# Turning rows of x by VectorE blocks and transfers within SBUF, in a hybrid decoder layer

## The chip, the core and the metric

The kernel runs on one core of a Trainium2 chip. The metric is the device time of one execution in microseconds (us), lower is better. TensorE (PE) multiplies and transposes, VectorE (DVE) and ScalarE (ACT) do elementwise work and empty PSUM, GpSimd (POOL) and SyncE (SP) mostly issue transfers (DMAs). SBUF is the memory on the chip with 128 partitions, PSUM the accumulator memory of TensorE.

## What is computed

The reference is one decoder layer on x, 2048 tokens by 1024 channels in float32:

```python
h = _rmsnorm(x, norm1_w)
proj = h @ w_in                                  # 1024 -> 3840 columns
o_hg = _hgrn2_mixer(...)                         # 4 heads of 128: gated linear recurrence over tokens
o_rw = _rwkv7_mixer(...)                         # 8 heads of 64: recurrence with a data-dependent decay
x = x + concatenate([o_hg, o_rw]) @ w_out
x = x + _conv_ffn(_rmsnorm(x, norm2_w), w_up, conv_w, conv_b, w_down)
out = _rmsnorm(x, final_norm_w)
```

The change touches the first line alone: how h reaches the layout in which TensorE multiplies it with w_in. That product needs channels on the partitions and tokens along the free dimension, while x lies in memory with one token per row.

## The kernel before

**Stages.** The first stage (up to about 1300 us) does the first norm, the input projection, both recurrences and the output projection of token blocks 0 to 2. The second does the rest. The change lies in the first stage, in the function `phase1`.

**Blocks.** The 2048 tokens are four blocks of 512 (`NBLK`, `BLK`). `KD` is 8: the 1024 channels are eight groups of 128. For each block, `hh` and `hl` hold the normed and turned h as a high and a low part, 128 channels by 512 tokens for each of the eight groups k. A projection of 128 columns is 8 x 3 matmuls (`mm3`, L270 to L272) into one PSUM bank of the kind "pj", of which there are two.

**Three streams.** `dense()` yields the projections, `rw_stream()` the rwkv recurrence (units `rw_super`, two per block) and `hg_stream()` the hgrn2 heads (`hg_unit`). A loop takes one step of each recurrence and then fills with 2000 ns of dense work, by the costs that `dense()` yields. So the program's order comes about. A planner then puts each engine's instructions in order: of those that are ready by its own costs it takes the one that comes first in the program. Each engine and each queue afterwards runs its list strictly in that order.

**The job list.** `dense()` builds a list of jobs: for each block a mark ("A"), then 30 projections ("P"), and ahead of blocks 2 and 3 the output projection of block 0 and 1 ("O"). `at[nb]` is the place of the mark of block nb. Into this list go extra jobs, at places counted from `at[nb]`: "E" jobs, which only issue work and cost nothing in the count, and jobs that yield costs. For the next block these are

- at +18 `load4`: four transfers of 128 rows of x (512 KB each) into `rows[nb]`, a tile "xt" of 128 partitions x 4 x 1024, one buffer;
- at +22 `norm4`: sums of squares (ScalarE, into a "wraw" buffer) and scaling of the rows (VectorE, L431);
- at +25 the job "T", `turn`: for each k four transposes of 128x128 on TensorE (L443) into a "pj" bank, which ScalarE copies back in place over the rows of `rows[nb]`, so that the tile then holds channels on its partitions.

In the last projection of the block (block 0), or in the last quarter of the output projection that follows it, `next_block` calls `split_h` for each k (L451, L452): the turned rows times the norm's weights, split into `hh` and `hl`.

**Block 0** is turned another way (`transposed`, with eviction straight into `hh`), at the start. Rows of x1 for the second norm (keys `("N", nb)`) also come through `load4` and are turned by `transposed`.

**Buffers that matter.** The pool `wp` has four buffers "wraw" of 2 KB per partition. In block 0 the weights pass through them: each projection loads two raw tiles of w_in (L568, issued by POOL), ScalarE and VectorE split them into "wh" and "wl", and POOL stores the split weights to memory (`Win`), from where later blocks load them without "wraw". The norm's squares, the rows of h for the second norm and the raw w_out tiles of the output projection use "wraw" too.

**SP's queue.** `dma` issues on SP. In the first stage SP carries, besides the loads of x: in each `rw_super` the transfers of `KBT` (16), `Ed` (4), `E` (2) and `RHS` (16), the first and last of which finish turns that VectorE began with 32x32 block transposes (L754, L765); the stores of the mixers' outputs to `oT`; and in the output projections the loads of `oT` ("oraw", L388) and x and the stores of x1. The step-by-step solve in `rw_super` (L804, L806) waits for `E`.

Of the kernel before, what the change touches and what calls it, by code (L numbers as in the profile page):

```python
# [7 lines left out]
F32 = mybir.dt.float32  # L8
# [3 lines left out]
AF = mybir.ActivationFunctionType  # L12
# [6 lines left out]
P = 128  # L19
T = 2048  # L20
D = 1024
KD = D // P
BLK = 512
# [44 lines left out]
def tile_layer(ctx, tc, consts, x, norm1_w, w_in, hg_lb_logits, hg_norm_w, rw_shift_mu, rw_w0, rw_w2,  # L68
# [4 lines left out]
    V, S, TE = nc.vector, nc.scalar, nc.tensor  # L73
# [40 lines left out]
    def act(out_, in_, func, **kw):  # L114

        want = tables.get(func)
        if want is not None and want != tab["now"]:
            pre = S.preload_act_table_set(want)
            for u_ in tab["uses"]:
                tc.add_manual_dep(pre.ins, u_.ins.name, NOSYNC, reason="table order")  # L120
            tab.update(now=want, pre=pre, uses=[])
        i_ = S.activation(out_, in_, func, **kw)  # L122
        if want is not None:
            tc.add_manual_dep(i_.ins, tab["pre"].ins.name, NOSYNC, reason="table order")
            tab["uses"].append(i_)
        return i_
# [147 lines left out]
    def phase1(c1):  # L274
# [22 lines left out]
        def bank(kind):  # L297
            return ps.tile([P, 512], F32, tag=kind, name=kind, bufs=2)
# [121 lines left out]
        def load4(key, src, r0):  # L420
            def f():
                rows[key] = row_tile()
                for i in range(4):
                    dma(rows[key][:, i, :], src[r0 + i * P:r0 + (i + 1) * P, :])
            return f

        def norm4(key):
            def f():
                for i in range(4):
                    t_ = rows[key][:, i, :]  # L430
                    V.tensor_scalar_mul(t_, t_, rstd(wp, t_, "nst", "wraw", 4))  # L431
            return f
# [1 line left out]
        def four_tiles(t_):  # L434
            return [t_[:, i, :] for i in range(4)]

        def turn(nb):

            t_ = rows[nb]
            for k in range(KD):  # L440
                tp = bank("pj")
                for i in range(4):
                    TE.transpose(tp[:, i * P:(i + 1) * P], t_[:, i, k * P:(k + 1) * P], ident)  # L443
                act(t_[:, :, k * P:(k + 1) * P], tp.rearrange("p (i t) -> p i t", i=4), AF.Copy)
                yield 436

        def split_h(nb, k):

# [67 lines left out]
        def dense():  # L516

            rows[0] = first
            jobs = []
            for nb in range(NBLK):  # L520
                if nb >= 2:
                    jobs.append(("O", nb - 2))
                jobs.append(("A", nb))
                jobs.append(("P", 3584, ev_lora(nb), lambda nb=nb: done["rw1"] >= 2 * nb, None))
                for s_ in range(2):
                    if s_ == 1:
                        jobs.append(("P", 3712, ev_gd(nb), lambda nb=nb: done["rw2"] >= 2 * nb, None))
                    n_rw = 2 * nb + s_
                    for u in range(3):
                        for p in (2 * s_, 2 * s_ + 1):  # L530
                            jobs.append(("P", 2048 + u * 512 + p * P, ev_rkv(nb, p, u),
                                         lambda n=n_rw: done["rw1"] >= n,
                                         mark("rw") if (u == 2 and p == 2 * s_ + 1) else None))
                    for j in (2 * s_, 2 * s_ + 1):
                        n_hg = 4 * nb + j
                        for i, ev in enumerate((ev_q, ev_f, ev_v, ev_g)):
                            jobs.append(("P", i * 512 + j * P, ev(nb, j), lambda n=n_hg: done["hg"] >= n - 1,
                                         mark("hg") if i == 3 else None))
            jobs.append(("O", 2))


            at = [i for i, jb in enumerate(jobs) if jb[0] == "A"]
            extra = []
            for nb in range(NBLK):
                if nb + 1 < NBLK:
                    extra += [(at[nb] + 18, ("E", load4(nb + 1, x[0], (nb + 1) * BLK))),
                              (at[nb] + 22, ("E", norm4(nb + 1))), (at[nb] + 25, ("T", nb + 1))]
                if nb >= 2:
                    extra += [(at[nb] + 6, ("E", load4(("N", nb - 2), x1d[nb - 2], 0))),
                              (at[nb] + 10, ("E", norm4(("N", nb - 2)))), (at[nb] + 11, ("N", nb - 2))]  # L550
            for m in range(2):
                extra += [(at[3] + 14 + 5 * m, ("E", sum_load(m))), (at[3] + 17 + 5 * m, ("E", sum_make(m)))]
            extra += [(at[3] + 25 + m, ("W", 2, o_take(m))) for m in range(4)]
            for i, jb in sorted(extra, key=lambda e: e[0], reverse=True):
                jobs.insert(i, jb)
            cols = [jb[1] for jb in jobs if jb[0] == "P"]
            NCOL = len(cols) // NBLK
            Win = [[[dp.tile([P, 4, P], F32, name=f"Win{ct}{k2}{c}") for c in "hl"] for k2 in range(2)]
                   for ct in range(NCOL)]
            loaded = {}  # L560

            def load(i):
                if i < len(cols) and i not in loaded:
                    ws, ct = [], cols[i] // P
                    for k2 in range(2):
                        if i < NCOL:
                            raw = wp.tile([P, 4, P], F32, tag="wraw", name="wraw", bufs=4)
                            wload(raw, w_in[0, k2 * 512:k2 * 512 + 512, cols[i]:cols[i] + P].rearrange("(k p) c -> p k c", p=P))  # L568
                            ws.append(split(wp, raw, [P, 4, P], "w", 4))
                            for c in range(2):  # L570
                                nc.gpsimd.dma_start(Win[ct][k2][c], ws[k2][c].bitcast(F32))
                        else:
                            ws.append(tuple(wp.tile([P, 4, P], F32R, tag="w" + c, name="w" + c, bufs=4) for c in "hl"))
                            for c in range(2):
                                wload(ws[k2][c].bitcast(F32), Win[ct][k2][c])
                    loaded[i] = ws

            i = 0
            load(0)
            ahead = iter(())  # L580
            for n, jb in enumerate(jobs):
                if jb[0] == "E":
                    jb[1]()
                    continue
                if jb[0] == "A":
                    if jb[1] == 0:
                        banks = spread()
                        ahead = transposed(four_tiles(rows[0]), "n1", lambda: next(banks), to_h)
                    continue
                if jb[0] == "T":  # L590
                    yield from turn(jb[1])
                    continue
                if jb[0] == "N":
                    yield from transposed(four_tiles(rows.pop(jb)), "n2", lambda: bank("pj"), to_h2(jb[1]))
                    continue
                if jb[0] in "OW":
                    while done["rw2"] < 2 * jb[1] + 2 or done["hg"] < 4 * jb[1] + 4:
                        yield None
                    if jb[0] == "W":
                        jb[2]()  # L600
                    else:
                        yield from (out_block(2, *rows["O"]) if jb[1] == 2 else out_block(jb[1], then=jb[1] + 2))
                    continue
                _, col, ev, cond, fin = jb
                while not cond():
                    yield None
                load(i)
                ws = loaded.pop(i)
                if i == 0:
                    next(ahead)  # L610
                    next(ahead)
                    constants()
                load(i + 1)
                i += 1
                acc = bank("pj")
                then = jobs[n + 1][1] if jobs[n + 1][0] == "A" else None
                for k in range(KD):
                    wh, wl = ws[k // 4]
                    next(ahead, None)
                    mm3(acc, (wh[:, k % 4, :], wl[:, k % 4, :]), (hh[:, k, :], hl[:, k, :]), k == 0, k == KD - 1)  # L620
                    if k == KD - 1:
                        ev(acc)
                        if fin is not None:
                            fin()
                    next_block(then, k)
                    yield 648
# [1000 lines left out]
```

## Time and profile before

| | |
|---|---|
| Median of 3 runs | 2648.05 us (2644.51 to 2653.97) |
| The profiled execution | 2645.14 us, span 2643.1 us |
| Granted TensorE clock, mean | 0.992 |
| Busy share of PE, DVE, ACT, POOL | 96%, 75%, 51%, 14% |
| First stage, 0 to 1300 us: busy us of PE, DVE, ACT, POOL | 1223.06, 909.86, 640.94, 364.77 |
| Transfers issued on SP for KBT and RHS, each | 128 |

Lines of the profile read as follows. In a timeline a line gives the start in us, the length in us, the engine, the line of the program, the operation, what is written and read, how many were merged, and in brackets the idle time before it and what ended that. The queue of an engine has a q behind its name (SPq): a line there is the issue of a transfer and not the transfer itself. In a list of groups the numbers are the shortest, median and longest length in ns, and the starts of the first and the last. Busy TensorE isn't TensorE at its peak, since matmuls overlap: their ends are modelled.

### The profile page before, as it was taken

Reading aid. Unit: us, or ns where it says so; the run is one execution under the profiler, and the core shown is the slowest. Engines: PE = TensorE matmul, PEld = TensorE weight load, DVE = VectorE, ACT = ScalarE, POOL = GpSimd, SP = SyncE. Lnnn points to the kernel's source line nnn. Section 1 sums busy time; section 2 is a strip of 40 time slices with the busy share of each in tenths; the row PEclk is TensorE's granted clock in tenths of the full one; section 3 lists DMA queues with packets and bytes.
Section 4 is the critical chain, followed back from the end, with each engine's and each line's share of the span. In section 5 each row is a group of like instructions: output and inputs, shape, how many; then the busy total and the mean of one; then the engine's idle time right before and its main releaser. Section 6 shows DMA issues by size and latency. Waiting matters only on the chain. (4 is left out here: it accounts for less than half of the span.)

```text
span 2643.1 us, 51079 instructions
## 1 busy us (share of the span) xinstructions
PE 2545.1 (96%) x19403; PEld 2044.3 (77%) x19403; DVE 1973.0 (75%) x3760; ACT 1356.5 (51%) x2242; POOL 381.1 (14%) x686
## 2 busy tenths in 40 slices
PE   7999999999999899999899999999999999999998
PEld 5877777767777667777678888787888887888887
DVE  4978576676676765787678799987998887766556
ACT  5565444555445554354466754556554544545444
POOL 6433222212222122232100000000000000000000
PEclk9999999999999999999999999999999999999999
DMA  8847464656665566856574477747764553998665
GB/s 305 243 161 204 141 173 128 149 152 212 191 180 145 168 212 184 262 167 164 188 260 136 129 233 255 230 152 228 245 204 130 169 172 128 337 318 280 204 192 187
DMA packets 415115, 523.18 MB, mean 198 GB/s; under 512 B 149280, under 2 KB 245910, under 8 KB 414870
## 3 DMA queue, kind: packets, MB, share of 16 engines
q1 hardware_dynamic: 360337, 341.59, 41.3%
q0 software_dynamic: 54464, 178.32, 21.1%
q8 instruction: 152, 2.49, 0.4%
q14 instruction: 94, 0.76, 0.1%
q10 hardware_dynamic: 68, 0.02, 0.0%
HBM read 372.99 MB, written 134.22 MB: 192 GB/s over the span
## 5 line engine op out<-in xcount | busy, mean ns | idle before, releaser
L270 PE MATMUL pj<-hh,wh 128*128 128x512 f32 x960 | 392.3, 409 | 4.7 <-ACT rkv L122 2.1
L271 PE MATMUL pj<-hl,wh 128*128 128x512 f32 x960 | 379.1, 395 | 0.0
L272 PE MATMUL pj<-hh,wl 128*128 128x512 f32 x960 | 378.3, 394 | 0.0
L270 PE MATMUL ua<-Bh,uwh 128*128 128x512 f32 x704 | 276.9, 393 | 6.7 <-ACT m L122 5.8
L272 PE MATMUL ua<-Bh,uwl 128*128 128x512 f32 x704 | 274.5, 390 | 0.0
L271 PE MATMUL ua<-Bl,uwh 128*128 128x512 f32 x704 | 274.3, 390 | 0.0
L270 PEld LDWEIGHTS pj<-hh,wh 128*128 128x128 f32 x960 | 181.2, 189 | 53.7 <-issue 9.0
L272 PEld LDWEIGHTS pj<-hh,wl 128*128 128x128 f32 x960 | 181.3, 189 | 39.3 <-issue 0.3
L271 PEld LDWEIGHTS pj<-hl,wh 128*128 128x128 f32 x960 | 181.5, 189 | 35.1 <-issue 0.6
L254 ACT CAST uwh<-uraw 128x512 fp32r<-128x512 f32 x220 | 134.1, 617 | 128.7 <-PE ua L271 54.1
L255 DVE TENSOR_TENSOR dal<-draw,dah 128x512 fp32r<-128x512 f32 x138 | 95.4, 691 | 107.0 <-ACT dah L254 106.7
L255 DVE TENSOR_TENSOR uwl<-uraw,uwh 128x512 fp32r<-128x512 f32 x220 | 147.6, 687 | 33.7 <-ACT uwh L254 33.6
L254 ACT CAST dah<-draw 128x512 fp32r<-128x512 f32 x138 | 85.6, 621 | 159.2 <-PE da L271 74.0
L270 PEld LDWEIGHTS ua<-Bh,uwh 128*128 128x128 f32 x704 | 132.2, 188 | 38.3 <-ACT m L122 10.6
L272 PEld LDWEIGHTS ua<-Bh,uwl 128*128 128x128 f32 x704 | 132.2, 188 | 28.0 <-DVE uwl L255 0.4
L271 PEld LDWEIGHTS ua<-Bl,uwh 128*128 128x128 f32 x704 | 132.3, 188 | 26.7
L270 PE MATMUL ud<-Bh,uwh 128*128 128x512 f32 x352 | 138.1, 392 | 0.0
L1497 POOL DMA_DIRECT2D gd<-y x2 | 1.1, 540 | 947.9 <-DVE y L1495 947.9
L272 PE MATMUL ud<-Bh,uwl 128*128 128x512 f32 x352 | 137.2, 390 | 0.0
L271 PE MATMUL ud<-Bl,uwh 128*128 128x512 f32 x352 | 137.1, 390 | 0.0
L271 PE MATMUL da<-dbl,dah 128*128 128x512 f32 x332 | 129.5, 390 | 0.2 <-DVE dbl L255 0.2
L272 PE MATMUL da<-dbh,dal 128*128 128x512 f32 x332 | 129.3, 389 | 0.0
(581 smaller groups left out, 6191.6 us busy)
## 6 DMA issues: line engine op xcount, KB each, us to landing
uraw<-in_w_up_dram SPq DMA_DIRECT2D x176, 256.0 KB
woraw<-in_w_out_dram POOLq DMA_DIRECT2D x96, 256.0 KB, 3.4
br<-gd SPq DMA_DIRECT2D x88, 256.0 KB
draw<-Sg SPq DMA_DIRECT2D x88, 256.0 KB
draw<-Tw SPq DMA_DIRECT2D x88, 256.0 KB
gd<-y SPq DMA_DIRECT2D x86, 256.0 KB
Sg<-br SPq DMA_DIRECT2D x72, 256.0 KB
xt<-x1d SPq DMA_DIRECT2D x32, 512.0 KB
```

The lines of the kernel that those rows point to most:

```text
L254: S.copy(hi, src)
L255: V.tensor_sub(lo, src, hi.bitcast(F32))
L270: TE.matmul(acc, lh, rh, start=first, stop=False, skip_group_check=skip)
L271: TE.matmul(acc, lh, rl, start=False, stop=False, skip_group_check=skip)
L272: TE.matmul(acc, ll, rh, start=False, stop=last, skip_group_check=skip)
L1497: (dma if end is None else nc.gpsimd.dma_start)(gd_[2 * h + b][fb * P:(fb + 1) * P, :], ys[0][:, b * BLK:(b + 1) * BLK])
```

## The change

For token blocks 1 to 3 the job "T" is gone. The rows are loaded in another arrangement: partition 32 g + t, slot i holds token 128 g + 32 i + t of the block, so each of the four transfers of `load4` now goes to 32 partitions with four rows each. The sums and the scaling of `norm4` are as before, row by row. For each k an "E" job does one block transpose on VectorE (128 partitions x 512, 32x32 blocks, into a "wraw" buffer called "turned") and then 16 transfers on SP, each of 32 partitions x 512 bytes, from "turned" back in place into `rows[nb]`. Two such jobs stand ahead of each of the projections at +24 to +27; by the way in which they are put into the list the order is k = 1, 0, 3, 2, 5, 4, 7, 6. `split_h` then reads the same tile in the same form as before.

```diff
         def load4(key, src, r0):
             def f():
                 rows[key] = row_tile()
-                for i in range(4):
-                    dma(rows[key][:, i, :], src[r0 + i * P:r0 + (i + 1) * P, :])
+                if isinstance(key, tuple):
+                    for i in range(4):
+                        dma(rows[key][:, i, :], src[r0 + i * P:r0 + (i + 1) * P, :])
+                    return
+                v = src[r0:r0 + BLK, :].rearrange("(g i t) d -> g t i d", g=4, i=4)
+                for g in range(4):
+                    dma(rows[key][g * 32:g * 32 + 32], v[g])
             return f
...
-        def turn(nb):
-
-            t_ = rows[nb]
-            for k in range(KD):
-                tp = bank("pj")
-                for i in range(4):
-                    TE.transpose(tp[:, i * P:(i + 1) * P], t_[:, i, k * P:(k + 1) * P], ident)
-                act(t_[:, :, k * P:(k + 1) * P], tp.rearrange("p (i t) -> p i t", i=4), AF.Copy)
-                yield 436
+        def turn(nb, k):
+
+            def f():
+                v = rows[nb][:, :, k * P:(k + 1) * P]
+                y = wp.tile([P, 4, 4, 32], F32, tag="wraw", name="turned", bufs=4)
+                V.transpose(y.rearrange("p c i t -> p i c t"), v.rearrange("p i (c t) -> p i c t", t=32))
+                for c in range(4):
+                    for g in range(4):
+                        dma(v[32 * c:32 * c + 32, g, :], y[32 * g:32 * g + 32, c].rearrange("p i t -> p (i t)"))
+            return f
...
                     extra += [(at[nb] + 18, ("E", load4(nb + 1, x[0], (nb + 1) * BLK))),
-                              (at[nb] + 22, ("E", norm4(nb + 1))), (at[nb] + 25, ("T", nb + 1))]
+                              (at[nb] + 22, ("E", norm4(nb + 1)))]
+                    extra += [(at[nb] + 24 + k // 2, ("E", turn(nb + 1, k))) for k in range(KD)]
...
-                if jb[0] == "T":
-                    yield from turn(jb[1])
-                    continue
```

## The prediction

> **What bounds the kernel now.** I read the page first, then the busy time of the first stage, where all of the change lies, then TensorE's timeline at the three places where rows of x are turned.
>
> ```profile
> span 2643.1 us, 51079 instructions
> PE 2545.1 (96%) x19403; PEld 2044.3 (77%) x19403; DVE 1973.0 (75%) x3760; ACT 1356.5 (51%) x2242; POOL 381.1 (14%) x686
> ```
>
> The stage with the recurrences ends near 1300 us; its row of the busy time by stretches (stretch, length, then PE, PEld, DVE, ACT, POOL, granted clock, DMA share):
>
> ```profile
> 0.00:1300.00 1300.00, 1223.06 (x13576) 959.21 (x13577) 909.86 (x2155) 640.94 (x1089) 364.77 (x656) 0.99 0.62 186
> ```
>
> TensorE is idle for 77 us of these 1300, so its own work is the bound, and time taken off it is a gain as long as the next wait isn't as long. The turns themselves, first all 96 transposes and their 24 evictions, then the timeline of TensorE at the three turns:
>
> ```profile
> L443 PE MATMUL pj<-ident,xt x96: 270/273/476, 210.3 to 836.5; 128*128 128x128 f32 x96
> L122 ACT ACTIVATE xt<-pj x24: 588/597/610, 213.6 to 836.8; 128x512 f32<-128x512 f32 x24
> ```
>
> ```profile
> 210.26 0.60 PE L443 MATMUL pj<-ident,xt 128*128 128x128 f32 x4
> 212.85 0.66 PE L443 MATMUL pj<-ident,xt 128*128 128x128 f32 x4 [1.99 <-ACT hf L122]
> 213.78 0.49 PE L1085 MATMUL rw<-part,group 128*128 128x512 f32 x1 [0.28 <-ACT part L247]
> 214.28 2.49 PE L443 MATMUL pj<-ident,xt 128*128 128x128 f32 x10
> ...
> 220.19 0.50 PE L270 MATMUL pj<-hh,wh 128*128 128x512 f32 x1 [0.20 <-ACT xt L122]
> ...
> 489.70 0.60 PE L443 MATMUL pj<-ident,xt 128*128 128x128 f32 x4
> ...
> 499.28 0.50 PE L270 MATMUL pj<-hh,wh 128*128 128x512 f32 x1 [0.25 <-ACT xt L122]
> ...
> 828.70 0.60 PE L443 MATMUL pj<-ident,xt 128*128 128x128 f32 x4
> ...
> 830.84 0.50 PE L1086 MATMUL rw<-part,group 128*128 128x512 f32 x1 [1.31 <-DVE part L248]
> ...
> 831.40 0.39 PE L1086 MATMUL rw<-part,group 128*128 128x512 f32 x1
> 831.63 1.03 PE L443 MATMUL pj<-ident,xt 128*128 128x128 f32 x8
> ...
> 836.49 0.48 PE L270 MATMUL pj<-hh,wh 128*128 128x512 f32 x1
> ```
>
> The reader is to see that a turn takes far longer than its matmuls. Eight transposes take 1.03 us, so 32 need about 4 us; yet from the first transpose to the projection's next matmul pass 9.93, 9.58 and 7.79 us. TensorE waits there for the two "pj" banks, which ScalarE empties late.
>
> **The change, part by part.** The working is against the profiled execution (span 2643.1 us, 2645.1 us with what lies around it); the median of the runs shown, 2648.05, is 2.9 us above it.
>
> *Removed from TensorE.* The three stretches sum to 27.3 us. Four sums for the rwkv stream (L1085, L1086) stand in each and stay, at 0.23 us from one start to the next (831.40 to 831.63): 12 x 0.23 = 2.8 us. So at most 24.5 us go. Some of the waits would come back: L1086 at 830.84 waited 1.31 us for VectorE's part, whatever is turned, and the same kind of wait can show elsewhere. If all waits came back, only the 96 transposes at 0.13 us (1.03 / 8) are saved, 12 us. The gain lies between 12 and 24.5; I take 22, as most waits are for banks that the turn itself fills. ScalarE loses 24 x 0.597 = 14 us; at 51% busy that alone is worth nothing beyond those waits.
>
> *Added on VectorE.* One 32x32 block transpose of 128x512 per 128 channels; the trace has the same shape:
>
> ```profile
> L765 DVE STREAM_TRANSPOSE ATb<-AR 128x512 f32<-128x512 f32 x16 | 10.9, 694 | 0.0
> 210.20:220.20 10.00, 7.28 (x38) 5.33 (x36) 9.75 (x11) 8.27 (x14) 3.67 (x6) 0.83 0.46 157
> ```
>
> 24 x 0.694 = 16.7 us, 5.6 per block. In block 1 they fall near the stretch in which VectorE is busy for 9.75 of 10 us, with the chain of the rwkv stream, so I charge 2 us; for blocks 2 and 3 VectorE has the rows of x ready long before (below) and fits them into idle time: nothing. If that cover is gone, it is 5.6 us each.
>
> *Added on SP's queue: the term that decides.* Each turn issues 16 transfers of 32 partitions x 512 bytes: 128 per block, 384 in all. No row shows that shape. The nearest are the transfers within SBUF from and to 32 partitions (KBT, RHS); then one to 64 partitions from memory, and the plain one of 128 partitions (times are shortest, median, longest issue in ns):
>
> ```profile
> L757 SPq DMA_DIRECT2D KBT<-KBb x128: 591/640/3207, 89.0 to 1201.6; - x128
> L770 SPq DMA_DIRECT2D RHS<-ATb x128: 585/610/2811, 116.2 to 1214.6; - x128
> L499 SPq DMA_DIRECT2D w2a<-in_rw_w_dram x1: 585/585/585, 11.6 to 11.6; - x1
> L1080 SPq DMA_DIRECT2D oT<-osq x12: 319/330/344, 142.5 to 966.5; - x12
> ```
>
> KBT has twice the pieces of RHS and costs 5% more, and the single-piece row of 64 partitions costs 585: so it isn't the pieces that cost, and 0.61 us is nearest, with about 0.05 between two. I take 0.66 us; the bounds are 0.37 (the 330 of L1080 with the same gap) and 0.96, from this row of the first RHS group beside the weights' loads:
>
> ```profile
> 116.19 15.36 SPq L770 DMA_DIRECT2D RHS<-ATb  x16
> ```
>
> A block's 128 transfers then hold SP for 84 us (47 to 123). The queue is in order, and the rwkv stream's own transfers go through it:
>
> ```profile
> 223.10 6.30 SPq L757 DMA_DIRECT2D KBT<-KBb  x8
> 234.69 2.02 SPq L745 DMA_DIRECT2D Ed<-M  x4
> 236.75 2.36 SPq L757 DMA_DIRECT2D KBT<-KBb  x2
> 240.11 1.33 SPq L748 DMA_DIRECT2D E<-Ed  x2
> 241.49 6.88 SPq L757 DMA_DIRECT2D KBT<-KBb  x6
> 248.47 12.74 SPq L770 DMA_DIRECT2D RHS<-ATb  x16
> ```
>
> These 38 take about 28 us without the waits between the groups. When are the rows ready, and when are they due? The rows are scaled by L431 and, once turned, split by L452; the load at 181.62 is the first that queues behind the first turn for a "wraw" buffer:
>
> ```profile
> L431 DVE TENSOR_SCALAR xt<-xt,nst x4: 747/748/878, 170.7 to 173.8; 128x1024 f32<-128x1024 f32 x4
> L431 DVE TENSOR_SCALAR xt<-xt,nst x4: 734/734/735, 421.5 to 423.5; 128x1024 f32<-128x1024 f32 x4
> L431 DVE TENSOR_SCALAR xt<-xt,nst x4: 751/752/754, 762.6 to 767.7; 128x1024 f32<-128x1024 f32 x4
> L452 DVE SCALAR_TENSOR_TENSOR hl<-xt,vt,hh x8: 744/748/752, 257.9 to 269.8; 128x512 fp32r<-128x512 f32 x8
> L452 DVE SCALAR_TENSOR_TENSOR hl<-xt,vt,hh x8: 744/747/753, 622.3 to 637.0; 128x512 fp32r<-128x512 f32 x8
> 181.62 0.76 POOL L568 DMA_DIRECT2D wraw<-in_w_in_dram  x1
> ```
>
> *Block 1* is ready at 174 us, but its turns take the four "wraw" buffers in turn with block 0's weights, so the first starts at about 182. Six turns go ahead of the KBT group and the last two behind RHS, by their places in the job list: 182 + 96 x 0.66 = 245; + 28 = 273; + 32 x 0.66 = 294; landing and split 4 (E starts 3.4 us after the last Ed issue ends, and a split takes 0.75) = 298. Due, as before, at 270.6 less the 9 us that TensorE no longer spends: 262. TensorE is 36 us late, with a few of the other streams' matmuls to fill it: most of those wait too, for E and RHS, which are late by the same queue. I charge 29. At 0.37 nothing or 9 is left; at 0.96 it is over 55. What is queued behind the waiting transfers: KBT, E and RHS; behind block transposes that wait for a buffer, all of VectorE; behind the buffers, the loads of block 0's last weights.
>
> *Blocks 2 and 3* have nearly 200 us from row to split (423 to 622), so 84 us of SP fit. But the last two turns still stand behind RHS and ahead of the output projection's loads:
>
> ```profile
> 538.45 15.45 SPq L388 DMA_DIRECT2D oraw<-oT  x4
> ```
>
> These come 32 x 0.66 = 21 us later. They wait for other things too (four take 15.45 us), so I charge 5 us each, 10 in all; bounds 0 and 21 each. The loads of x in four pieces of 32 partitions are due a hundred us after their issue: nothing.
>
> *Sum:* -22 + 2 + 29 + 10 = +19 us: 2645.1 becomes 2664, and on the median of the runs 2667.
>
> **Rivals.** *Faster (0.25): the issue is cheap.* If a single-piece transfer costs what L1080's does, 0.37 us a piece, block 1 is done at about 277 in the same order (RHS ends at 261 as now, then 32 x 0.37 and 4), 15 us late of which 9 count, or in time if the last pair is issued ahead of KBT; with -22 + 2 that leaves -11 to -20, so 2628 to 2637. The point that decides is (262 - 182 - 28 - 4) / 128 = 0.38 us per transfer: below it SP is done in time. For it speaks only the row of 128 partitions; against it all rows of 32 and 64. The Trainium skill, "DMA: Bandwidth & Descriptors" (Issuing engines are not separate DMA queues), says that the sequencer's time to initiate a DMA is usually small relative to the DMA itself; by that the turn would be hidden and the time 2628. The trace here disagrees with it for small transfers: 0.61 us of issue for 32 KB.
>
> *No change (0.15).* The other streams' matmuls fill the hole in block 1 better than I think: with 18 of the 36 us filled and the output projections on time, -22 + 2 + 18 = -2, so 2646. For it stands the row behind the first turn, without idle time on TensorE though E and RHS are still on their way:
>
> ```profile
> 220.20:257.00 36.80, 36.80 (x395) 30.40 (x398) 27.63 (x72) 9.30 (x17) 13.78 (x24) 1.00 0.81 212
> ```
>
> *Far slower (0.12).* SP keeps the 0.96 us of the first RHS group, since block 0's weights still load: block 1 ends at 182 + 128 x 0.96 + 32 + 4 = 341, 79 late, 60 after filling; the projections' loads are 31 us late, 12 charged each: +64 or more, 2712 and above. A clock that falls in such a hole adds to it: 0.83 was granted at 210 to 220, where TensorE worked 7.28 of 10 us, and 0.99 over the stage.
>
> **How the numbers follow.** About 0.3% (8 us) is what a measurement of this kernel can tell from no change. Forecast case (9 to 64 us slower) 0.48, far slower 0.12: slower 0.60. Same 0.15. Faster 0.25. The range goes from 2626, the full gain, which leaves out a third of the faster case (0.08), to 2712, which leaves out the far slower case: 0.20 outside. The forecast case's own range is 2656 to 2712.
>
> **What would show it.** Right: issues of 0.55 to 0.7 us for the new transfers; SP busy without a break from about 182 to 290; TensorE idle for tens of us before block 1's first projection, waiting for splits of "hh"; E and RHS of the first block's second half landing later than 241 and 261; no gap of the old kind at 210, 490 and 829. Wrong: issues under 0.4 us; TensorE without a hole before block 1; or the last turns issued ahead of KBT, with VectorE waiting for "wraw" buffers instead.

## The result and the profile after

| | before | after |
|---|---|---|
| Median, same chip, 4 runs each | 2648.11 us (2644.51 to 2653.97) | 2718.41 us (2716.02 to 2722.68) |
| Profiled execution, span | 2645.14 us, 2643.1 us | 2720.27 us, 2718.3 us |

The ratio is 1.0265, 95% interval 1.0241 to 1.0289: the change costs 70 us, where 19 were forecast and the range ended at 2712. The head of the page after:

```profile
span 2718.3 us, 51388 instructions
...
PE 2566.3 (94%) x19307; PEld 2051.8 (75%) x19307; DVE 1995.8 (73%) x3784; ACT 1347.9 (50%) x2220; POOL 381.7 (14%) x686
```

The busy time by stretches after, of the first stage and of two shorter pieces of it (columns as in the prediction; the granted clock is the last but two):

```profile
0.00:1300.00 1300.00, 1172.88 (x12453) 909.60 (x12456) 878.13 (x2044) 592.70 (x994) 351.91 (x631) 0.95 0.62 181
440.00:545.00 105.00, 87.71 (x1085) 65.82 (x1084) 60.12 (x120) 40.45 (x65) 21.82 (x40) 0.90 0.44 128
885.00:1000.00 115.00, 85.20 (x1080) 63.96 (x1081) 72.17 (x181) 35.56 (x65) 18.92 (x36) 0.84 0.55 146
```

The same two stretches before:

```profile
440.00:545.00 105.00, 100.87 (x1061) 78.84 (x1054) 71.13 (x170) 46.40 (x74) 24.25 (x45) 0.98 0.58 146
885.00:1000.00 115.00, 104.63 (x1157) 79.16 (x1158) 73.48 (x162) 59.50 (x102) 25.68 (x48) 1.00 0.57 190
```

No engine became fuller: PE, DVE, ACT and POOL are all emptier, and the DMA share of the stage is 0.62 as before. In the same 1300 us TensorE does 50 us less. So something makes all of them wait. The granted clock fell from 0.99 to 0.95 over the stage; in the sparse stretches to 0.90 and 0.84. In the first stage the trace grants 1.0 or 0.5 only, the latter in pieces of 3.4 us and its multiples (27.3 us from 946.0 on). The Trainium skill, "TensorE: Matmul & The Clock Gate" (Part 1), says that TensorE's clock is halved after an idle window of about 3.4 us; the trace agrees in the half and in the length, but the window needn't be empty: in the 3.4 us before 946.0 TensorE still worked for 1.1 us.

Where the time went is read off two marks. The first is the projections' own, the first eviction of each block (ScalarE's timeline, "tl", at the start of blocks 1, 2 and 3). Before:

```profile
278.24 0.67 ACT L122 ACTIVATE tl<-pj,omu 128x512 f32<-128x512 f32 x1
644.49 0.67 ACT L122 ACTIVATE tl<-pj,omu 128x512 f32<-128x512 f32 x1
979.47 0.67 ACT L122 ACTIVATE tl<-pj,omu 128x512 f32<-128x512 f32 x1
```

After:

```profile
285.03 0.68 ACT L122 ACTIVATE tl<-pj,omu 128x512 f32<-128x512 f32 x1
691.19 0.67 ACT L122 ACTIVATE tl<-pj,omu 128x512 f32<-128x512 f32 x1
1056.52 0.67 ACT L122 ACTIVATE tl<-pj,omu 128x512 f32<-128x512 f32 x1
```

Late by 6.8, 46.7 and 77.1 us. The second mark is the rwkv recurrence's: its first E transfers in blocks 1, 2 and 3 (SP's timeline). Before:

```profile
383.05 1.15 SPq L748 DMA_DIRECT2D E<-Ed  x2
...
715.46 1.15 SPq L748 DMA_DIRECT2D E<-Ed  x2
...
1048.75 1.15 SPq L748 DMA_DIRECT2D E<-Ed  x2
```

After:

```profile
405.34 1.70 SPq L752 DMA_DIRECT2D E<-Ed  x2
...
762.33 1.15 SPq L752 DMA_DIRECT2D E<-Ed  x2
...
1130.04 2.33 SPq L752 DMA_DIRECT2D E<-Ed  x2
```

Late by 22, 47 and 81 us: so block 1's turn costs 22 us, block 2's 25 and block 3's 34, and nothing more comes later. Of block 1's 22 us the projections show only 6.8 at first.

SP's queue after, first the group of the new transfers (shortest, median, longest issue in ns):

```profile
L450 SPq DMA_DIRECT2D xt<-turned x384: 507/589/2048, 184.2 to 925.9; - x192
```

Then SP's timeline from the first turn to the E transfers, and parts of it in the other two blocks:

```profile
184.25 26.12 SPq L450 DMA_DIRECT2D xt<-turned  x37
...
211.56 60.58 SPq L450 DMA_DIRECT2D xt<-turned  x91
272.25 2.61 SPq L749 DMA_DIRECT2D Ed<-M  x4
274.96 2.35 SPq L761 DMA_DIRECT2D KBT<-KBb  x2
279.46 1.15 SPq L752 DMA_DIRECT2D E<-Ed  x2
...
442.25 72.43 SPq L450 DMA_DIRECT2D xt<-turned  x102
...
526.11 0.52 SPq L945 DMA_DIRECT2D oT<-yo  x1
526.67 7.86 SPq L450 DMA_DIRECT2D xt<-turned  x9
...
879.84 46.61 SPq L450 DMA_DIRECT2D xt<-turned  x70
926.54 2.16 SPq L749 DMA_DIRECT2D Ed<-M  x4
```

All 128 transfers of a block go ahead of the second unit's Ed and E, not 96. SP is through at 272.1, 534.5 and 926.5 us, and E is issued at 279 instead of 240. The store of the mixer's output (oT from yo), ahead of which 119 transfers stand in block 2, is issued at 526 instead of 483. In block 2 Ed goes only at 555 (513 before), 21 us after SP is through: VectorE stood waiting for that store until 533 and wrote the last of M, which Ed moves, at 555.

Who waits (the list of waits, 440 to 600 us: engine, line, what ended the wait, us in total, times, longest):

```profile
POOL woraw L395 <- DMA xt<-turned: 29.6, 3, 11.7
...
DVE turned L447 <- DMA xt<-turned: 16.1, 4, 6.8
DVE KB L719 <- DMA oT<-yo: 12.4, 1, 12.4
...
DVE etmp L808 <- DMA E<-Ed: 6.1, 1, 6.1
...
PE pj L270 <- DMA wh<-Win140h: 4.9, 1, 4.9
```

VectorE's list stands still three times over: for a buffer of the turned tiles, for the buffer that KB shares with the stored yo, and for E. POOL's list stands for the same buffers, and behind its load of w_out stand the weights for TensorE (Win140h). POOL waited for these buffers before too: 53 us in this stretch for all their holders together, 48 after, so its wait isn't the new one.

### The profile page after: what moved, and what is told of

It reads as the page before. It is cut to its first block, busy times and chain, and to the rows that moved or that the text cites. A ratio compares the mean times of both kernels' runs of the same rounds, so it can differ in the third digit from the quotient of the medians.

```text
span 2718.3 us, 51388 instructions
## 1 busy us (share of the span) xinstructions
PE 2566.3 (94%) x19307; PEld 2051.8 (75%) x19307; DVE 1995.8 (73%) x3784; ACT 1347.9 (50%) x2220; POOL 381.7 (14%) x686
## 4 chain that ended last, share of the span: by engine, by line
PE 47%; DVE 9%; issue 7%; DMA 7%; ACT 2%; POOL 1%; SPq 1%; DVEq 0%; POOLq 0%; ACTq 0%
PE ua L270 4%; PE ua L272 4%; PE ua L271 4%; PE pj L270 3%; PE pj L272 3%; PE pj L271 3%; PE da L271 3%; PE da L272 3%; PE da L270 3%; PE ud L272 2%; PE ud L271 2%; PE ud L270 2%; PE db L272 2%; PE db L271 2%; PE db L270 2%
## 5 line engine op out<-in xcount | busy, mean ns | idle before, releaser
L272 PE MATMUL pj<-hh,wl 128*128 128x512 f32 x960 | 386.0, 402 | 5.1 <-DMA wl<-Win251l 1.6
L271 PE MATMUL pj<-hl,wh 128*128 128x512 f32 x960 | 383.1, 399 | 0.0
```

The costliest lines, as they stand in the source:

```text
L271: TE.matmul(acc, lh, rl, start=False, stop=False, skip_group_check=skip)
L272: TE.matmul(acc, ll, rh, start=False, stop=last, skip_group_check=skip)
```

## The experiments

The theory at this point, S: SP's time. 128 issues hold SP for 86 to 92 us a block, and the recurrence's stores and transfers behind them come late. Rivals: the shared buffers (B), the bytes (D), VectorE's turns (V). A median is given with its ratio to the kernel before in the same session. "gone" below is the kernel without any turn, 2643.25 us.

**1. Without the transfers.**

```diff
-                for c in range(4):
-                    for g in range(4):
-                        dma(v[32 * c:32 * c + 32, g, :], ...)
```

> The 16 transfers of each turn are left out (384 in all), so rows of blocks 1 to 3 stay turned only within their 32x32 blocks; VectorE's block transposes, their buffers and the split loads of rows stay. Theory S (the queue of SP: 128 issues a block at 0.59 us hold back the stores, the K transfers and the E and RHS transfers of the recurrence behind them; TensorE waits): all of the loss goes and the saved TensorE work shows, 2618 to 2636. Theory V (VectorE's 24 block transposes of 0.7 us, in a stretch where VectorE is full, or the loads in quarters): the time stays above 2690. Theories B (buffers of the weights shared with the turned tiles) and D (the traffic of the 64 KB of each group of four transfers) say as S does, so this run sets only V apart.

2649.60 us, ratio 1.0012 (0.9995 to 1.0029). The whole loss goes, so V falls. But no theory had said that the time would only come back to that of before: TensorE does no transposes here, and nothing is gained.

**2. Half of the transfers** (`for c in range(2)`).

> 8 of the 16 transfers of each turn are left out (channels 64 to 127 of each group of 128 are not put in their place). SP then has 64 issues a block, 38 us instead of 75. S: in block 1 the queue is through about 37 us earlier, that is ahead of the place where the recurrence's own transfers used to be issued (240 us and 248 us in the kernel before), and in blocks 2 and 3 likewise, so more than half of the loss goes: 2625 to 2655. D: the loss goes with the bytes, about half of the 90 us between this kernel without transfers and with them: 2665 to 2680. B: the buffers are held about half as long: 2660 to 2680.

2665.71 us, 1.0073 (1.0049 to 1.0097): the first 64 cost 16 us, the second 64 cost 53. That speaks for a threshold. The time lies within B's and D's figures and 11 us over S's.

**3. A quarter of the bytes** (each transfer moves 32 of 128 elements).

> Each of the 16 transfers of a turn moves only its first 32 of 128 elements per partition (128 B instead of 512 B; three quarters of the rows are not put in place). Number of issues, partitions, waits and buffers unchanged, a quarter of the bytes. S: the issue price does not go with the bytes, so 2705 to 2725, as the changed kernel. D: the loss goes with the bytes: 2640 to 2660. B: about as S, since the buffer is held until SP has issued its last transfer.

2712.20 us, 1.0248 (1.0228 to 1.0267); the issue's median is again 589 ns. D falls: leaving out three quarters of the bytes is worth 6 us.

**4. The mixers' stores on POOL** (`last_dma` returns POOL's queue for all blocks).

> Only the stores of the mixers' outputs (oT from yo and from osq) of blocks 0 to 2 go by POOL's queue instead of SP's. If the stores held up behind the turned transfers (VectorE waited 12.4 us for one before it could write KB in block 1's turn stretch) are what costs: 15 to 30 us come off, 2690 to 2705. If it is the K, E and RHS transfers further behind in the same queue: those are issued as late as before, 2712 to 2722. S says a mix: the first wait goes and the second ends last, 2700 to 2718.

2721.42 us, 1.0293 (1.0257 to 1.0328). Waits, 440 to 600 us:

```profile
DVE KB L719 <- DMA oT<-yo: 3.4, 1, 3.4
```

VectorE's wait for the store fell from 12.4 to 3.4 us and the time did not: another wait ended last. The time lies within the figure for the transfers further behind, and 3 us over S's.

**5. No turn at all.** From the kernel before:

```diff
-                              (at[nb] + 22, ("E", norm4(nb + 1))), (at[nb] + 25, ("T", nb + 1))]
+                              (at[nb] + 22, ("E", norm4(nb + 1)))]
```

> The kernel before with the job T left out and nothing in its place: rows of blocks 1 to 3 are loaded, normed and split, but not turned at all. Theory P (TensorE's turns lie on the path that sets the end, and what the kernel without the 16 transfers did not gain, 2650 instead of 2625, went into VectorE's block transposes and the loads in quarters): three turn stretches of 8 to 10 us go, 2618 to 2630. Theory F (TensorE's turns filled time that it would else have waited in: projections only run ahead of the recurrences and the wait comes later in the block): 2640 to 2650, with turn places 9 to 11 us shorter and about as much lost at the end of each block.

2643.25 us, 0.9983 (0.9971 to 0.9995). F holds: all of TensorE's turn is worth 4.5 us (0.17%), not 22. The blocks begin earlier, and then TensorE stands in front of the recurrence. ScalarE's timeline of this kernel:

```profile
269.56 0.69 ACT L122 ACTIVATE tl<-pj,omu 128x512 f32<-128x512 f32 x1
641.19 0.67 ACT L122 ACTIVATE tl<-pj,omu 128x512 f32<-128x512 f32 x1
983.39 0.67 ACT L122 ACTIVATE tl<-pj,omu 128x512 f32<-128x512 f32 x1
```

And a row of its TensorE timeline:

```profile
544.96 0.65 PE L823 MATMUL rw<-TZ,M 32*32 32x32 f32 x32 [5.52 <-DVE TZ L810]
```

Block 1 begins 8.7 us earlier than before, block 2 3.3 earlier, block 3 3.9 later. A wait of 5.52 us for the step-by-step solve is one of those that take the saved time, and the stage's mean clock is 0.97 against 0.99.

**6. The same transfers from a constant tile.**

```diff
-                        dma(v[32 * c:32 * c + 32, g, :], y[32 * g:32 * g + 32, c]...)
+                        dma(v[32 * c:32 * c + 32, g, :], ident[32 * g:32 * g + 32, :])
```

> The same 384 transfers at the same places in the queue, same sizes and shapes, but read from a constant tile (the identity matrix) instead of the block-turned tile, so that the buffers shared with the weights come free as soon as VectorE has written them; the rows are overwritten with the constant. S (the issues themselves on SP): 2708 to 2724, as the changed kernel. B (VectorE and the weights wait for buffers that the transfers hold): VectorE no longer waits in line for a buffer, most of the 70 us goes, 2650 to 2680.

2702.03 us, 1.0200 (1.0178 to 1.0222). Below S's figure by 6 us: letting the buffers go early is worth 16 us, not quite a quarter of the loss. B is a part, not the cause.

**7. The turn through memory.**

```diff
+                for g in range(4):
+                    dma(turn_d[nb % 2][k]...[g], y[32 * g:32 * g + 32]...)
+                dma(v, turn_d[nb % 2][k])
```

> The turn complete, but through memory: of each block-turned tile four stores of 32 partitions and one load of 128 partitions, 5 transfers instead of 16, 40 a block instead of 128. S: the loss follows the number of issues (64 a block cost 16 us over none, 128 cost 70): 2650 to 2665. If it is not the issues but that turned rows are late (the wait of the transfers themselves, here two in series): 2680 or more.

2652.80 us, 1.0014 (1.0004 to 1.0025): the whole turn with 40 issues a block instead of 128 costs 3 us over the kernel without transfers, though it moves every byte twice.

**8. The recurrence's transfers on POOL** (KBT, Ed, E, RHS: `dma` becomes `nc.gpsimd.dma_start`).

> The changed kernel with all its transfers, but the recurrence's own transfers (K, Ed, E, RHS; 38 for each unit of the rwkv recurrence) are issued by POOL instead of SP. S, with the recurrence as what is held back: E and RHS no longer stand behind 128 turned transfers, and most of the loss goes, 2655 to 2685 (POOL's loads of weights then stand behind them, which takes some of it). If what is held back is the rest (oraw, the stores, VectorE's buffers): 2710 to 2725.

2846.06 us, 1.0749 (1.0730 to 1.0768): far outside all figures. A row of its list of waits (180 to 600 us):

```profile
POOL wh L582 <- PE pj L272: 115.7, 39, 8.9
```

and the group of RHS issues, now on POOL:

```profile
L774 POOL DMA_DIRECT2D RHS<-ATb x128: 582/582/609, 113.1 to 1398.2; - x128
```

POOL's list waits for TensorE at each load of weights, since their buffers are in use (it did before: 198.2 us, 60 times); now the recurrence's transfers stand behind these loads and wait with them. The run says nothing of SP, and it is no way out.

**9 and 10. Transfers that wait for nothing.** On "gone", at the places of the change:

```diff
+                for c in range(4):          # range(2) in the second
+                    for g in range(4):
+                        dma(aside_d[nb - 1][k][c][g], rows[nb][32 * g:32 * g + 32, c, k * P:(k + 1) * P])
```

> The kernel with the job T left out (2643 us; rows are not turned), and at the places where the change puts its transfers the same number of them, 128 a block of 32 partitions x 512 B, but from the normed rows to a place in memory that nobody reads. Nothing waits for them, they hold none of the shared buffers, and VectorE turns nothing. Theory S (SP's time alone holds the recurrence's own transfers back): if an issue takes about 0.59 us here too, 2685 to 2705; if a transfer to memory is issued in 0.33 us, as the stores of the mixers' outputs are (42 us a block), 2650 to 2665. If SP's time is not the cause: 2640 to 2648.

> As the kernel of the 128 transfers to memory that nobody reads, with 64 of them a block. S with a threshold (SP has about 60 us free between the stores of the first unit and the K transfers of the second; 38 us or 21 us of issues fit): 2643 to 2655. S without a threshold, each issue costing alike: half of the loss of 128.

2647.78 us, 1.0004 (0.9990 to 1.0019), and 2644.71 us, 0.9979 (0.9964 to 0.9994). 384 issues cost nothing that can be measured, which seemed to end theory S. SP's group of the first:

```profile
L452 SPq DMA_DIRECT2D aside_d<-xt x384: 302/420/2182, 171.4 to 830.9; - x192
```

and its timeline:

```profile
200.79 41.62 SPq L452 DMA_DIRECT2D aside_d<-xt  x73
242.51 3.49 SPq L754 DMA_DIRECT2D Ed<-M  x4
```

The dose was not the same: an issue to memory took 420 ns, the queue began at 171 and was through at 242.4 instead of 272.1 (in the other two blocks at 485.0 and 831.2 instead of 534.5 and 926.5). What this run shows is that E may be 12 us late for nothing (250 against 238 us in "gone").

**11. Blocks 2 and 3 turned in the output projection** (`turn(then, j)` at every second step of `out_block`).

> The whole change, but the turns of blocks 2 and 3 are put into the output projection ahead of each block, two of its 32 steps apart, where SP has little to issue and no K, E or RHS transfer stands behind them; block 1 as in the change. S: the losses of blocks 2 and 3 (31 us each in the changed kernel against the one before) go to a large part, 2660 to 2685; block 1's stays. If the 128 issues cost wherever they stand, 2705 to 2725. Cost of the new place: loads and stores of the output projection, and its weights' buffers, now share with the turns.

2716.04 us, 1.0253 (1.0232 to 1.0275): no gain, and within the figure for a cost wherever they stand. Yet in block 1's stretch, now without a turn, nothing was lost any more: its two first E transfers go at 408.9 and 543.0, 26 and 25 us later than before, so block 1's turn alone costs about 25. The next is 45 us late again. One of POOL's waits, 575 to 690 us:

```profile
POOL woraw L395 <- DMA xt<-turned: 21.5, 4, 6.4
```

The loads of w_out there take the same four buffers as the turned tiles, and SP's loads and stores of the projection stand behind the transfers. POOL waits longer there for VectorE (40.3 and 25.8 us in its two largest rows). The cost moved to the other place; which of these makes it isn't shown.

**12. TensorE's turn three projections later** (`at[nb] + 28`, from the kernel before).

> The kernel before with its TensorE turn three projections later in the block (job T at +28 instead of +25), where ScalarE is idle for more than half of the time. If the turn's 8 to 10 us of TensorE a block were spent waiting for ScalarE's evictions and on the path: 2630 to 2640. Theory F (the turn fills time in which TensorE would else wait; without any turn it is 2643): 2640 to 2652, no gain to be had here.

2640.70 us, 0.9975 (0.9963 to 0.9987): the only complete version under both kernels, by 6.6 us, at the edge of what can be told. It lies at the border of the two answers, and by the intervals it can't be told from leaving the turn out altogether (4.5 us). Turns and the projection's next matmul, TensorE's timeline:

```profile
232.76 0.60 PE L443 MATMUL pj<-ident,xt 128*128 128x128 f32 x4
...
240.22 0.50 PE L270 MATMUL pj<-hh,wh 128*128 128x512 f32 x1
...
843.06 0.60 PE L443 MATMUL pj<-ident,xt 128*128 128x128 f32 x4
...
849.07 0.48 PE L270 MATMUL pj<-hh,wh 128*128 128x512 f32 x1
```

Where ScalarE is free the turn takes 7.46 and 6.01 us instead of 9.93 and 7.79.

**13 and 14. Turning earlier.** The whole change, then the turn through memory, at other places:

```diff
-  (at[nb] + 18, load4) (at[nb] + 22, norm4) (at[nb] + 24 + k // 2, turn)
+  (at[nb] + 12, load4) (at[nb] + 14, norm4) (at[nb] + 15 + k, turn)
```

> The whole change, all 384 transfers, but each block's rows are loaded at +12, normed at +14 and turned one k for each of the projections +15 to +22 (instead of +18, +22 and two k for each of +24 to +27), so that the 75 to 88 us of issues begin right behind the RHS transfers of the first unit and end ahead of the K, Ed and E transfers of the second. Theory Q (the issues cost only because they begin at 184, 442 and 840 us, too late to be through before the second unit's transfers at 240, 508 and 848 us, so that E and RHS come 30 to 45 us late): most of the 70 us over the kernel without transfers goes, 2650 to 2672. Theory W (VectorE's block transposes and the buffers that they share with the weights, wherever the turn stands): 2695 to 2720.

> The turn through memory (5 transfers for each k instead of 16) at the earlier places (load +12, norm +14, turns +15 to +22). Without any turn the kernel takes 2643 us, with block transposes alone 2650 us, with the turn through memory at the later places 2653 us. Q: nothing left to be late, 2642 to 2653. W: as at the later places or above, 2650 to 2665, since VectorE and the weights' buffers are as busy there.

2706.96 us, 1.0233 (1.0212 to 1.0254), and 2679.12 us, 1.0130 (1.0115 to 1.0145). Q's figure is missed by 35 us, and W's (VectorE's block transposes and the shared buffers, wherever the turn stands) is met. The turn through memory, harmless at its old place, costs 26 us here, 14 more than W's figure. So the earlier places have a price of their own: both kernels are 16 to 19 us behind "gone" already at block 1's first projection, and lose again where block 3's rows are loaded. One row of SP there, in the first of the two:

```profile
758.05 25.52 SPq L774 DMA_DIRECT2D RHS<-ATb  x16
```

16 RHS issues take 25.52 us instead of the 12.74 of the first group in the turn stretch of the kernel before. In the first of the two SP is through with block 1's transfers at 216.7 us, long ahead of Ed, and the first E of block 1 still goes at 400.0 instead of 383.1: there 17 us are lost though the queue isn't late. In the other two blocks the transfers end at 514.5 and 896.3 us, late again for the store. Why the early places cost isn't settled, and W isn't ruled out for them.

**15 and 16. Side by side, and one behind the other.** The block transposes as in the change, and its transfers to memory that nobody reads; they read the normed rows in the first, the block-turned tile in the second:

```diff
-                        dma(v[32 * c:32 * c + 32, g, :], y[32 * g:32 * g + 32, c]...)
+                        dma(aside_d[nb - 1][k][c][g], rows[nb][...])     # e15
+                        dma(aside_d[nb - 1][k][c][g], y[32 * g:32 * g + 32, c]...)     # e16
```

> VectorE's 24 block transposes as in the change, and 128 transfers a block on SP as in the change, but the transfers read the normed rows, which are there before the block transposes, and go to a place in memory that nobody reads: the two parts are side by side and neither waits for the other (rows are not turned further). If the cost of the change is that its transfers stand in SP's queue waiting for VectorE's block transposes and hold its buffers meanwhile: 2648 to 2662, the kernel with block transposes alone being at 2650. If SP's 75 us a block and VectorE's block transposes cost together what neither costs alone, for example because their traffic meets: 2685 to 2715.

> As the kernel with the two parts side by side, with one difference: each transfer reads the block-turned tile instead of the normed rows (and still goes to memory that nobody reads). So each stands in SP's queue until VectorE has made its tile, and holds a buffer shared with the weights until it is through. Cost by the wait and the held buffers: 2700 to 2722, the changed kernel's time, though nothing waits for what is moved. Cost by the way back into the rows (the split waiting for turned rows): 2650 to 2670.

2647.34 us, 1.0019 (1.0006 to 1.0032), at the first answer's lower end, and 2666.66 us, 1.0084 (1.0057 to 1.0111). With the wait for VectorE's tiles come 19 us, and 52 more with the rows in SBUF as the target. The second time lies within the figure of the way back, and 33 us under that of the wait and the held buffers. But with the way back SP is also through later; that is what the last two runs take apart.

**17 and 18. Target and time apart.** On "gone", 128 transfers a block from the constant tile into the rows; and experiment 16 with 21 transfers for each k instead of 16:

```diff
+                        dma(v[32 * c:32 * c + 32, g, :], ident[32 * g:32 * g + 32, :])     # e17
...
-                for c in range(4): for g in range(4): dma(aside_d[...], y[...])
+                for j in range(21): dma(aside_d[nb - 1][k][j], y[...])     # e18
```

> The kernel without any turn (2643 us), and 128 transfers a block on SP that write into the rows in SBUF as the change's do, but from a constant tile: nothing is turned by VectorE, no shared buffer is held, and the transfers can begin once the rows are normed (172, 416 and 762 us where transfers to memory did). Issue price expected 0.59 us with 0.04 us between, 80 us a block, against 0.42 us and some 60 us to memory. Theory S (how late SP's queue is through): about 252, 500 and 845 us, so E is late by 15 to 20 us in the first block alone: 2648 to 2665. If writing to SBUF from 128 small transfers costs by itself, whenever it ends (by the difference between 2718 and 2667 us): 2690 or more.

> The kernel whose transfers read the block-turned tiles and go to memory that nobody reads (2667 us with 16 for each k), with 21 for each k: 168 a block at about 0.48 us a step are 80 us, the SP time of the change's 128 into SBUF at 0.63 us. S (SP's time behind the block transposes): 2705 to 2725, as the changed kernel. If the way back into SBUF makes the other 51 us: 2668 to 2680.

2689.75 us, 1.0156 (1.0140 to 1.0171), and 2700.44 us, 1.0193 (1.0172 to 1.0214). The first, over S's 2665 and at the edge of the rival's 2690: its group on SP:

```profile
L452 SPq DMA_DIRECT2D xt<-ident x384: 507/589/2261, 173.2 to 882.6; - x192
```

its timeline on SP:

```profile
213.15 50.66 SPq L452 DMA_DIRECT2D xt<-ident  x73
263.92 2.27 SPq L754 DMA_DIRECT2D Ed<-M  x4
```

and waits in the first stage (0 to 1300 us), two of VectorE's and two of TensorE's:

```profile
DVE KB L724 <- DMA oT<-yo: 29.1, 3, 16.9
...
DVE etmp L813 <- DMA E<-Ed: 17.9, 3, 13.4
...
PE rw L1095 <- DVE part L248: 28.5, 5, 16.4
PE hg L1055 <- DVE Ti L815: 13.3, 1, 13.3
```

The same 73 transfers take 50.66 us into SBUF and 41.62 us to memory, 0.69 against 0.57 each, and SP is through 21 us later. Only the split waits for them (1.9 us), no shared buffer is held, and yet VectorE stands for E, and for the store that lets KB's buffer go, and TensorE stands for VectorE: 16.4 us in the stretch with the longest wait for the store, 13.3 us for the solve that waits for E. VectorE's two waits are 47 us, where experiment 9 has 12.7 for E and none for the store; the times of the two kernels differ by 42. The second, 5 us under S's figure and 20 over the rival's: 40 more transfers a block to memory, which nobody reads, cost 34 us. SP's timeline in 16:

```profile
201.28 53.23 SPq L451 DMA_DIRECT2D aside_d<-turned  x91
```

and in 18:

```profile
203.71 68.06 SPq L451 DMA_DIRECT2D aside_d<-turned  x131
```

With SP through at 271.8 us, as in the changed kernel (272.1), 2700 of its 2718 us are there without the way back into SBUF. The agreement is one of the sums, though, and partly luck: by the first E of blocks 1, 2 and 3 against experiment 1 the three turns cost 32, nothing and 16 us here, and 20, 21 and 28 in the changed kernel. Block by block the two lose in different places.

Put in the order of when SP is through with block 1's transfers, most of the runs tell one story:

| kernel | transfers a block | SP through, us | first E issued, us | median, us | ratio |
|---|---|---|---|---|---|
| 5, no turn | 0 | | 237.7 | 2643.25 | 0.9983 |
| 10, to memory, no wait | 64 | 209.0 | 236.8 | 2644.71 | 0.9979 |
| 15, side by side | 128 | 240.4 | 247.0 | 2647.34 | 1.0019 |
| 9, to memory, no wait | 128 | 242.4 | 250.0 | 2647.78 | 1.0004 |
| 2, half | 64 | 246.5 | 258.3 | 2665.71 | 1.0073 |
| 16, behind, to memory | 128 | 254.5 | 260.9 | 2666.66 | 1.0084 |
| 17, into SBUF, no wait | 128 | 263.8 | 268.0 | 2689.75 | 1.0156 |
| 3, a quarter of the bytes | 128 | 270.3 | 276.3 | 2712.20 | 1.0248 |
| 18, behind, to memory | 168 | 271.8 | 282.5 | 2700.44 | 1.0193 |
| 6, from a constant | 128 | 272.5 | 277.7 | 2702.03 | 1.0200 |
| the change | 128 | 272.1 | 279.5 | 2718.41 | 1.0265 |

In these runs the transfers are free up to about 242 us; from there to 272 us, 30 us later, the time rises by 52 us over three blocks. Block 1's end stands here for all three blocks, though in the changed kernel block 1 makes less than a third of the loss. Experiments 13 and 14 don't fit the row (216.7 and 190.2 us, 2707 and 2679). At the same end the change lies 16 to 18 us above 6 and 18. Against 6 that is the price of the held buffers; against 18, whose tiles are held too, for shorter, it isn't separated further.

## Why the prediction was right or wrong

- *The direction, and the price of an issue: right.* Issues of 589 ns, forecast at 0.61 us; 128 held SP for 86 to 92 us, forecast at 84. So the rival of the cheap issue fell for the reason given; to memory, at 420 ns and with nothing to wait for, the same count was free. The Trainium skill, "DMA: Bandwidth & Descriptors" (Issuing engines are not separate DMA queues), says that the time to initiate a DMA is usually small relative to the DMA itself. Here it was 0.59 us of the 2.5 from issue to landing (median), and it was not the single issue but 128 in one queue that counted.
- *Removed from TensorE, -22: wrong.* The stretches of 27 us were read as time on the path because TensorE is 94% busy in the stage, and "most waits are for banks that the turn itself fills". Of the 7.2 us in which TensorE was idle in the three stretches only about 1.3 were for such banks (xt in the lines); 4.1 were for the projection's own eviction ahead of the turn (hf). Without any turn the kernel is 4.5 us faster. The turn stood in front of work that would wait for the recurrence anyway; the sum should have asked what is late next, as it did for SP. Off by 18 us.
- *VectorE, +2.* Block transposes and loads in quarters together cost 6 us (2649.60 against 2643.25). Off by 4.
- *SP, block 1, +29, and blocks 2 and 3, +10: the step that failed most.* Together +39, measured 69 (2718.41 against 2649.60). By the first E of blocks 1, 2 and 3 against experiment 1 (384.9, 720.6 and 1060.5 us there) block 1's turn cost 20 us where 29 were charged, and those of blocks 2 and 3 cost 21 and 28 where 5 each were. For these two only the turns behind RHS were charged; the turns ahead of it, 75 us of SP begun at 442 and 840 us with E due at 518 and 855 before, were costed at nothing because the rows themselves are due 100 us later. What stands behind them falls due meanwhile: in block 2 the store went at 483 and E at 518 before. Block 1's size came out near by luck: the order was another (all eight turns went ahead of Ed and E, not six, the sign named under "wrong", and with it VectorE's waits for buffers), and ahead of block 1's first projection only 6.8 us were lost, not 36, because what is late is not the split but E, which the recurrence needs. The 38 transfers of the recurrence taken at 28 us are 31.6 by the lines shown; that changes little.
- *A store overlooked.* The prediction named KBT, E, RHS and oraw as queued behind the turns. It didn't name oT from yo, though it stood in the list of SP's work: it lets go a buffer that VectorE needs for KB. In experiment 17 that wait alone is 29 us; in the changed kernel it is 12.4, and taking the stores off SP (experiment 4) gained nothing by itself.
- *The clock* was named only in the far slower rival, by the row of 0.83; the stage's mean fell to 0.95. How much of the 70 us it makes can't be told apart from the waits that bring it: "gone" has 0.97 and loses nothing.
- *The sum:* -4.5 + 6 + 69 = 71, against -22 + 2 + 39 = 19. Of the 52 us between them, 18 lie in the gain, 4 in VectorE's term and 30 in SP's. Within SP's 69, the held buffers make some 16 (experiment 6) and the issues in the queue the rest; how the rest splits between E and the store isn't shown.

## What to carry to other kernels

Before a step is moved to a queue, write down what stands behind it in that queue, stores included, with the time at which each is due, and the time at which the step can begin: here the queue was free as long as it was through about when the recurrence's own transfers were due, and dear beyond that, for transfers that nobody read as for the real ones. Few large transfers beat many small ones even by a detour: 5 instead of 16 for each k took the loss from 70 to 4 us. And a busy engine's time is a gain only if its next work is ready: leave the work out altogether once, and see.

## What the runs showed of the hardware

- Issuing on SP a transfer of 32 partitions x 512 bytes took 589 ns into SBUF and 420 ns to memory (shortest 507 and 302), and was the same for 128 bytes a partition as for 512.
- On POOL the issue of an RHS transfer took 582 ns, near SP's 610.
- The mean clock of the stage without any turn is 0.97 with the time unchanged: a lower granted clock can be the mark of a wait and no loss by itself.
